# Ragged self-attention: a size class of 340 rows between 352 and 320

## The chip, the cores and the metric

The kernel runs on one core of a Trainium2 chip. The metric is the device time of one execution in microseconds (us); three runs of the kernel before took 351.78, 352.02 and 353.03 us, the median being 352.02 us. A separate execution was profiled; it took 353.66 us, of which 351.8 us lie between its first and its last instruction (the span).

The engines are called as in the profile: PE (TensorE, matmuls), DVE (VectorE), ACT (ScalarE), POOL (GpSimd), SP (SyncE, which here only starts transfers). PSUM is the memory that matmuls write to.

## The reference

A batch of 32 sequences, each of its own length between 64 and 511 rows, goes through one self-attention layer with 8 heads of 64. Rows beyond a sequence's length are zero in the output.

```python
for b in range(batch):                      # 32
    seq_len = lengths[b]
    x_b = x[b, :seq_len]                    # seq_len x 512
    q, k, v = np.split(np.matmul(x_b, w_qkv), 3, axis=-1)
    ...                                     # 8 heads of 64
    scores = 0.125 * np.matmul(q, k.transpose(0, 2, 1))
    attn = np.exp(scores - scores.max(-1, keepdims=True))
    attn = attn / (attn.sum(-1, keepdims=True) + 1e-08)
    output[b, :seq_len] = np.matmul(attn, v)...
```

The lengths are drawn with a fixed seed. Sorted, they are 502, 447, 446, 436, 363, 357, 351, 347, 343, 333, 323, 315, 310, 261, 260, 257, 246, 230, 223, 220, 216, 183, 164, 152, 143, 140, 134, 119, 101, 86, 79, 75.

## The kernel before, in words

**Sorting and classes.** At the start the kernel ranks the sequences by length, longest first, and takes them in pairs: ranks 0 and 1, 2 and 3, and so on, 16 pairs. A pair is worked with one code body, built for a class of N rows; the class is the smallest one that holds the longer sequence of the pair. The classes (`CLASSES`, L26) are the 15 multiples of 32 from 512 to 64. A table of the 16 pairs' classes is made on DVE (`class_table`, L881): it counts for each pair how many thresholds (all classes but the largest, written by POOL into `thr_f`, L1326) are not below its length. Each engine then reads its next class from that table (`next_class`, L923) and branches to the body.

With the lengths above the 16 pairs of the kernel before fall into the classes 512, 448, 384, 352, 352, 352, 320, 288, 256, 224, 224, 192, 160, 160, 128, 96. Pairs are numbered from 0 here, so pairs 3, 4 and 5 are the three of class 352; pair 5 holds the lengths 323 and 315, and pair 6, of class 320, the lengths 310 and 261.

**One half of a body.** A body has two halves, one for each sequence of the pair (`half`, L564). While PE does the attention of one sequence, it projects the next one between its steps, so each half holds the work of two sequences:

- Q0 to Q3 and K0 to K3 (small letters where ACT instead of DVE empties the bank): one of the four pairs of heads, 4 matmuls of N columns each (`qk`, L362);
- V: the value projection, here 4 matmuls of 512 columns for each of the T row tiles of 128 (`vtile`, L429);
- scores and their exponential, in one of two forms below;
- A0 to A3: attention times values, 18 matmuls of 65 columns for a pair of heads where T is 3 (`attnv`, L451), normalised by DVE into `onat`, which ACT and SP store.

What is projected in a half has W columns: N where the next sequence is of the same class, the next lower class where the kernel leaves the class (`leave`, L916).

**The two forms of scores where T is 3.** The ordinary form (`S` in the order string of L555, `scores`, L281) makes one key block of 128 keys at a time: two matmuls of N columns, one for each head of the pair, into one of two PSUM slots, then one exponential of 2N elements per partition on ACT. A half has 12 such steps. The dense form (`D` in L558, `scores_dense`, L325) lays all three key blocks of a head side by side in 1024 columns of PSUM, so 3N must not exceed 1024; both slots together hold a pair of heads. It makes 8 matmuls (each block that crosses the 512-column bank boundary is cut in two), then one exponential of 3N elements for each head. A half has 4 such steps. `is_dense` (L662) decides:

```python
def is_dense(N):
    return -(-N // P) == 3 and 3 * N <= 2 * MAXS      # P = 128, MAXS = 512
```

In the kernel before it holds for 320 and 288, not for 384 and 352. Each dense step first waits until ACT has emptied both slots; an ordinary step waits for its own slot alone.

**Code paths.** `graph` (L952) writes, for each class and engine, the blocks lead, first, again, last and tail. `first` holds the first half; a branch then goes to `again` (next pair of the same class, second half with W = N, back to `first`) or to `last` (second half with W of the next lower class, then `tail`, which branches to the lead of a lower class, or straight to `first` two classes down). On PE some of these blocks are put at chosen places within 256 instructions (`align`, L966), and branches get hints which way they will go. SP and POOL walk a plain chain of compares (`loops`, L941).

**Transfers.** SP starts, for each sequence, a load of its rows into `x_nat`; POOL casts to f16; SP starts one transposing DMA per row tile into `xT` (`to_xT`, L1160); PE waits on `s_xt` for them before it projects (`start_proj`, L570). Zeros for rows beyond the class's tiles are written from `zt`, also by SP.

Of the kernel before, what the change touches and what calls it, by code (L numbers as in the profile page):

```python
# [13 lines left out]
P = 128  # L14
# [5 lines left out]
STEP = 32  # L20
# [2 lines left out]
SECOND = {4: 20, 3: 60, 2: 0, 1: None}  # L23
AT_DENSE = 45
PIECE = 222
CLASSES = [STEP * k for k in range(16, 1, -1)]  # L26
FETCH = 256


# [109 lines left out]
def kernel(  # L139
# [9 lines left out]
    B, MAXS, D = x.shape  # L149
# [7 lines left out]
    def sb(name, shape, dt):  # L157
        return nc.alloc_sbuf_tensor(name, shape, dt).ap()
# [27 lines left out]
    rk_f = sb("rk_f", [B, NR], FP32)  # L186
    thr_f = sb("thr_f", [1, B // 2, len(CLASSES) - 1], FP32)
    ident_f = sb("ident_f", [P, P], FP32)
# [476 lines left out]
    def make_body(N, W, last=False):  # L665

        T = -(-N // P)
        pr = Prog(CANON, 0)
        st = {"slot": 0, "bank": 0}
        for h in range(2):  # L670
            st["x"] = False
            pr.add("dve", lambda e: set_now(e))
            half(pr, h, T, N, (N, W)[h], st, last and h == 1)
            pr.add("dve", lambda e: e.reg_add(rank_reg[0], rank_reg[0], 1))
            if h == 0:
                pr.second = {g: len(ops) for g, ops in pr.ops.items()}
        assert st == {"slot": 0, "bank": 0, "x": True}
        for b in banks:
            if not pr.busy[b]:
                pr.add("pe", lambda e, b=b: e.sem_inc(free[b], 1))  # L680
        assert not pr.signals
        return pr
# [3 lines left out]
    def set_now(e):  # L686
        rv = e.snap(rank_reg[0], min_val=0, max_val=B - 1)
        now[0] = masks[:, bass.ds(rv, 1), :, :].rearrange("p o a t -> p (o a) t")

    def make_bridge():  # L690
        pr = Prog(CANON, 0)
        acquire(pr, "a0")
        acquire(pr, "s1")
        pr.signals.append(s_xtf[0])
        scores(pr, 1, 0, 0, 0, 1, P)
        pr.add("pe", lambda e: e.sem_inc(free["a0"], 1))
        return pr

    def make_settled():

        pr = Prog(CANON)
        acquire(pr, "a1")
        pr.add("pe", lambda e: e.sem_inc(free["a1"], 1))
        return pr
# [176 lines left out]
    def class_table(e):  # L881
        q = Chain(e, s_self)
        q.tensor_tensor(
            out=thr_f,
            in0=n_s[0:1, 0:B:2].unsqueeze(2).broadcast_to([1, B // 2, len(CLASSES) - 1]),
            in1=thr_f, op=ALU.is_le,
        )
        q.reduce_sum(out=cls_f, in_=thr_f, axis=mybir.AxisListType.X)
        q.tensor_copy(out=cls[:, 0 : B // 2], in_=cls_f)
        q.memset(cls[:, B // 2 : B // 2 + 2], len(CLASSES))  # L890
        q.signal(s_cls)
# [21 lines left out]
        q.signal(s_tab)  # L913

    stay = {N: make_body(N, N) for N in CLASSES}
    leave = {N: make_body(N, max(N - STEP, CLASSES[-1])) for N in CLASSES}  # L916
    final = {N: make_body(N, max(N - STEP, CLASSES[-1]), True) for N in CLASSES if N <= P}
    bridge, settled = make_bridge(), make_settled()
    prologue = make_prologue()

# [2 lines left out]
    def next_class(e):  # L923
        r, k = regs[e.engine]
        e.reg_add(r, r, 1)
        if e.engine == nc.tensor.engine:
            k = regs["next"]
        e.reg_load(k, cls[0:1, bass.ds(e.snap(r, min_val=0, max_val=B // 2 + 1), 1)])

    def begin_loops(e):  # L930
        e.wait_ge(s_cls, 1)
        r, k = e.alloc_register("pair"), e.alloc_register("cls")
        e.reg_mov(r, 0)
        e.reg_load(k, cls[0:1, 0:1])
        regs[e.engine] = (r, k)
        if e.engine == nc.tensor.engine:
            regs["next"] = e.alloc_register("next")
            e.reg_add(r, r, 1)
            e.reg_load(regs["next"], cls[0:1, 1:2])

    def loops(e, name, body):  # L941
        r, cur = regs[e.engine]
        for k, N in enumerate(CLASSES):
            top = nc.cur_bb
            lab, out_ = f"{name}_b{k}", f"{name}_x{k}"
            e.br_cmp(cur, k, lab, out_, "IS_EQ")
            nc.switch_bb(lab, parent=top)
            body(e, N)
            e.br_cmp(cur, k, lab, out_, "IS_EQ")
            nc.switch_bb(out_, parent=top)  # L950
# [136 lines left out]
    def wait_dec(e, s, n=1):  # L1087
        e.wait_ge(s, n)
        e.nop().then_inc(s, -n)  # L1089
# [39 lines left out]
    with nc.Block() as block:  # L1129

        @block.sync
        def _(e):
# [27 lines left out]
            def to_xT(h, N):  # L1160
                T = -(-N // P)
                for t in range(T):
                    tile_to_xT(h, t, min(P, N - t * P))
                if T < NT:
                    e.nop().then_inc(s_xt[h], 16 * (NT - T))

            def tile_to_xT(h, t, n):
                e.dma_start_transpose(
                    out=xT[h][:, :, t * P : t * P + n], in_=x16[h][0:n, t, :]
                ).then_inc(s_xt[h], 16)  # L1170
# [141 lines left out]
        @block.gpsimd  # L1312
        def _(e):
            def iota(o, pattern, base, mult, last=False):
                ins = e.iota(o, pattern=pattern, base=base, channel_multiplier=mult,
                             allow_small_or_imprecise_dtypes=True)
                if last:
                    ins.then_inc(s_iota, 1)

            iota(pos_f, [[-1, B]], B - 1, 0)  # L1320
            iota(pos_c, [[0, 1]], B - 1, -1)
            iota(rk_f[:, 0:B], [[1, B]], 0, 0)
            iota(rk_f[:, B:NR], [[0, NR - B]], B - 1, 0)
            iota(sel[:, 1, :], [[0, P]], 0, 1)
            iota(row_f, [[P, NT]], 0, 1)
            iota(thr_f, [[0, B // 2], [-32, len(CLASSES) - 1]], CLASSES[0] - 32, 0, True)  # L1326
            q = Chain(e, s_pself)
            q.memset(ident_f, 0.0)
            q.affine_select(
                out=ident_f, in_=ident_f, compare_op=ALU.not_equal, fill=1.0,  # L1330
                base=0, pattern=[[-1, P]], channel_multiplier=1,
            )
            q.join()
            e.tensor_copy(out=ident, in_=ident_f).then_inc(s_id, 1)
            rank = e.alloc_register("rank")
            e.reg_mov(rank, 0)

            def cast(h, T):
                wait_dec(e, s_xl[h], 16)
                e.tensor_copy(out=x16[h][:, 0:T, :], in_=x_nat[h][:, 0:T, :]).then_inc(  # L1340
                    s_xc[h], 1
                )

            def ones(h, T, src):
                e.tensor_copy(  # L1345
                    out=v_aug[h][:, 0:T, :, HD],
                    in_=src[:, 0, 0:T].unsqueeze(2).broadcast_to([P, T, NH]),
                ).then_inc(s_on[h], 1)

            def fill(i, a):  # L1350
                e.memset(ep32[:, i, a], 0.01).then_inc(s_ini, 1)  # L1351


            e.wait_ge(s_c0[NT - 1], 1)
            fills = [(i, a) for i in range(1, NPAIR) for a in range(2)]
            for i, a in fills:
                fill(i, a)
            for t in range(2):
                e.wait_ge(s_x1[t], 16)
                e.tensor_copy(out=x16[1][:, t, :], in_=x_nat[1][:, t, :]).then_inc(s_xc[1], 1)  # L1360
            e.wait_ge(s_tab, 1)
            ones(0, NT, masks[:, B, :, :])
            e.wait_ge(s_c1[NT - 1], 1)
            e.memset(qkT[1].bitcast(FP32)[:, 1 : 2 * NPAIR : 2, :], 0.0).then_inc(s_ini, 1)
            e.wait_ge(s_tab, 2)
            wait_dec(e, s_x16f[0])
            cast(0, NT)
            begin_loops(e)

            def body(e, N):  # L1370
                T = -(-N // P)
                for h in range(2):
                    wait_dec(e, s_vf[1 - h])
                    rv = e.snap(rank, min_val=0, max_val=B - 1)
                    ones(1 - h, T, masks[:, bass.ds(rv, 1), :, :].rearrange(
                        "p o a t -> p (o a) t"))
                    wait_dec(e, s_x16f[1 - h])
                    cast(1 - h, T)
                    if h == 0:
                        next_class(e)  # L1380
                    e.reg_add(rank, rank, 1)

            loops(e, "pool", body)
# [89 lines left out]
```

## Time and profile before

| what | value |
|---|---|
| runs, us | 351.78, 352.02, 353.03 (median 352.02) |
| profiled execution, us | 353.66 |
| its span, us | 351.8 |
| PE busy | 332.7 us, 95% of the span |
| ACT busy | 246.4 us, 70% |
| DVE busy | 198.7 us, 56% |
| POOL busy | 60.4 us, 17% |
| mean granted TensorE clock | 0.990 |

"Busy" is the time in which an engine has an instruction under way. A row of the costliest groups gives line, engine, operation, output and input tiles, shape and count, then busy time and the mean of one instruction, then the idle time of the engine just ahead of them and what ended it. A table of stretches gives the busy time of each engine between two moments of the span. A row of the timeline gives the start, the time taken, the instructions merged into it and, in brackets, the idle time before it.

### The profile page before, as it was taken

The numbers are of one execution on the slowest core, as the hardware profiler recorded it, in microseconds if no ns is written. First come the engines' busy times: TensorE is split into PE (matmuls) and PEld (weight loads), VectorE is DVE, ScalarE is ACT, GpSimd is POOL, SyncE is SP. The second block draws the span as 40 slices with busy tenths as digits, with TensorE's granted clock in tenths as the row PEclk, the third lists the DMA queues.
The fourth block names the chain that finished last, engine by engine and source line by source line (L and its number), as shares of the span: only waits on it lengthen the run. The fifth ranks groups of instructions, "written<-read, shape, count | busy, mean of one in ns | idle before, by whom it ended". The sixth has DMA issues, their size and how long they took to land. (4 is left out here: it accounts for less than half of the span.)

```text
span 351.8 us, 11327 instructions
## 1 busy us (share of the span) xinstructions
PE 332.7 (95%) x3982; PEld 203.5 (58%) x3983; DVE 198.7 (56%) x442; ACT 246.4 (70%) x355; POOL 60.4 (17%) x90
## 2 busy tenths in 40 slices
PE   7799999999999999999999999999999999996972
PEld 2565445555545565555555566667677777664751
DVE  3576566666645445354354555655756667664652
ACT  4468778777768888988888877788675766553431
POOL 2534020202010111011011022201121122120120
PEclk9999999999999999999999999999999999999898
DMA  6957989866677496897678679899799687765632
GB/s 206 346 138 265 276 273 253 244 212 167 204 174 259 110 314 229 160 308 263 175 251 303 168 211 311 248 254 170 200 196 197 178 177 196 175 199 167 130 107 68
DMA packets 83462, 74.57 MB, mean 212 GB/s; under 512 B 40640, under 2 KB 63168, under 8 KB 83392
## 3 DMA queue, kind: packets, MB, share of 16 engines
q1 hardware_dynamic: 71536, 62.15, 65.6%
q10 hardware_dynamic: 11856, 11.54, 9.6%
q8 instruction: 37, 0.61, 0.8%
q14 instruction: 33, 0.27, 0.2%
HBM read 27.80 MB, written 36.70 MB: 183 GB/s over the span
## 5 line engine op out<-in xcount | busy, mean ns | idle before, releaser
L321 ACT ACTIVATE ep<-psc 128x704 f16<-128x704 f32 (+7 forms) x217 | 172.4, 845 | 61.9 <-PE psc L279 46.2
L279 PE MATMUL pa<-xT,w_r 128*128 128x352 f16 (+14 forms) x1056 | 155.3, 281 | 7.7 <-PEq L55 6.1
L279 PEld LDWEIGHTS pa<-xT,w_r 128*128 128x128 f16 x1056 | 83.7, 99 | 54.2 <-issue 22.5
L388 DVE CAST qkT<-pa 128x512 f16<-128x512 f32 (+8 forms) x96 | 54.2, 566 | 70.9 <-PE pa L279 70.4
L279 PE MATMUL pa<-w_r,xT 128*128 128x512 f16 (+2 forms) x384 | 83.2, 349 | 0.3 <-DVE v_aug L443 0.3
L279 PE MATMUL pav<-v_aug,ep 128*128 128x65 f16 x1792 | 77.4, 194 | 0.0
L279 PEld LDWEIGHTS pav<-v_aug,ep 128*128 128x128 f16 x1792 | 70.0, 98 | 11.9 <-issue 1.7
L279 PE MATMUL psc<-qkT 64*128 64x352 f16 (+14 forms) x686 | 65.8, 291 | 1.1 <-ACT ep L321 0.5
L443 DVE TENSOR_TENSOR v_aug<-pa,masks 128x512 f16<-128x512 f32 (+1 forms) x76 | 51.4, 677 | 22.2 <-PE pa L279 19.8
L386 ACT CAST qkT<-pa 128x352 f16<-128x352 f32 (+6 forms) x92 | 41.8, 454 | 21.4 <-ACTq L55 14.4
L524 DVE SCALAR_TENSOR_TENSOR onat<-pav,masks,rcp 128x256 f32<-128x256 f32 (+2 forms) x128 | 52.0, 444 | 5.4 <-DVE rcp L500 1.6
L1345 POOL CAST v_aug<-masks 128x24 f16 (+4 forms) x33 | 9.1, 276 | 255.7 <-POOLq L1089 255.7
L279 PEld LDWEIGHTS pa<-w_r,xT 128*128 128x128 f16 x384 | 31.4, 98 | 32.1 <-issue 6.6
L1340 POOL CAST x<-x_nat 128x1536 f16<-128x1536 f32 (+3 forms) x33 | 42.1, 1275 | 14.3 <-POOLq L1089 14.1
L279 PEld LDWEIGHTS psc<-qkT 64*128 64x128 f16 x686 | 23.1, 94 | 34.5 <-issue 29.1
L500 DVE RECIPROCAL rcp<-pav 128x8 f32<-128x8 f32 (+1 forms) x68 | 14.6, 214 | 37.0 <-PE pav L279 21.3
L353 ACT ACTIVATE ep<-psc 128x864 f16<-128x864 f32 (+2 forms) x32 | 27.7, 918 | 7.6 <-PE psc L279 6.5
L522 DVE TENSOR_TENSOR onat<-pav,rcp 128x512 f32<-128x512 f32 (+2 forms) x32 | 17.8, 558 | 1.1
L708 PE MATMUL psc<-zt 128*128 128x512 f16 x22 | 7.5, 499 | 1.7 <-DVE zt L1405 1.7
L778 ACT CAST w_r<-w_f 128x512 f16<-128x512 f32 (+1 forms) x6 | 4.4, 758 | 4.2 <-DMA w_f<-in_w_qkv_dram 4.2
L1351 POOL MEMSET ep<- 128x1024 f32 x6 | 5.4, 955 | 9.1 <-DVE x L769 9.1
L708 PEld LDWEIGHTS psc<-zt 128*128 128x128 f16 x22 | 2.4, 119 | 4.7 <-issue 2.4
(59 smaller groups left out, 35.4 us busy)
## 6 DMA issues: line engine op xcount, KB each, us to landing
out_dram<-zt SPq DMA_DIRECT2D x16, 768.0 KB, 6.1
x_nat<-in_x_dram SPq DMA_DIRECT2D x12, 768.0 KB, 5.0
x_nat<-in_x_dram SPq DMA_DIRECT2D x7, 1024.0 KB, 5.8
x_nat<-in_x_dram SPq DMA_DIRECT2D x11, 512.0 KB, 4.3
out_dram<-onat ACTq DMA_DIRECT2D x12, 384.0 KB, 5.4
out_dram<-onat SPq DMA_DIRECT2D x12, 384.0 KB, 3.9
out_dram<-onat ACTq DMA_DIRECT2D x16, 256.0 KB, 4.2
out_dram<-zt SPq DMA_DIRECT2D x12, 256.0 KB, 4.4
```

The lines of the kernel that those rows point to most:

```text
L279: return lambda e: e.matmul(o, lhsT, rhs, start=start, stop=stop)
L321: lambda e: e.activation(out=dst, in_=src, func=AF.Exp, scale=scale),
L353: lambda e, par=par, b=b: e.activation(out=ep[:, i, par, 0:3, 0:N], in_=psc_f[:, par, 0 : 3 * N].rearrange("p (t n) -> p t n", n=N), func= ...
L386: group(pr, b, eng, mms, lambda e: e.copy(out=dst, in_=src))
L388: group(pr, b, eng, mms, lambda e: e.tensor_copy(out=dst, in_=src))
L443: lambda e: e.tensor_tensor(out=v_aug[h][:, t, lo // HD : lo // HD + n, 0:HD], in0=pa[:, bank, 0:w].rearrange("p (a d) -> p a d", d=HD), i ...
L500: pr.add("dve", lambda e: e.reciprocal(out=rv, in_=den).then_inc(s_r, 1))
L522: ins = e.tensor_tensor(op=ALU.mult, **ops)
L524: ins = e.scalar_tensor_tensor(scalar=now[0][:, 1, t : t + 1], op0=ALU.mult, op1=ALU.mult, **ops)
L708: e.matmul(psc[:, 1, 0, :], zt16[:, 0:P], zt16[:, 0:MAXS], start=True, stop=True)
L1340: e.tensor_copy(out=x16[h][:, 0:T, :], in_=x_nat[h][:, 0:T, :]).then_inc(s_xc[h], 1)
L1345: e.tensor_copy(out=v_aug[h][:, 0:T, :, HD], in_=src[:, 0, 0:T].unsqueeze(2).broadcast_to([P, T, NH]),).then_inc(s_on[h], 1)
```

## The change

A sixteenth class of 340 rows is put between 352 and 320. 340 is the largest N for which 3N (1020) fits 1024 columns, so `is_dense` holds for it. With it:

- pair 5 (lengths 323 and 315) goes to class 340 instead of 352. No other pair changes its class: the next lower pair, with 310, stays in 320;
- the second half of pair 4, which stayed in class 352 and projected 352 columns, now leaves the class and projects 340; the two halves of pair 5 take the dense form, the first projecting 340 columns and the second 320;
- the next lower class of each class is looked up in a table (`lower`) instead of N - 32;
- transposes still move a multiple of 32 rows (96 in the last tile of 340, as for 352), so their number and sizes stay;
- the thresholds are written by three iota instructions on POOL instead of one, since their spacing is no longer even; the table has 16 x 15 entries instead of 16 x 14;
- every engine gets the code of one more class.

```diff
-CLASSES = [STEP * k for k in range(16, 1, -1)]
+DENSE_ROWS = 340
+CLASSES = sorted([STEP * k for k in range(2, 17)] + [DENSE_ROWS], reverse=True)
...
     stay = {N: make_body(N, N) for N in CLASSES}
-    leave = {N: make_body(N, max(N - STEP, CLASSES[-1])) for N in CLASSES}
-    final = {N: make_body(N, max(N - STEP, CLASSES[-1]), True) for N in CLASSES if N <= P}
+    lower = dict(zip(CLASSES, CLASSES[1:] + CLASSES[-1:]))
+    leave = {N: make_body(N, lower[N]) for N in CLASSES}
+    final = {N: make_body(N, lower[N], True) for N in CLASSES if N <= P}
...
             def to_xT(h, N):
                 T = -(-N // P)
                 for t in range(T):
-                    tile_to_xT(h, t, min(P, N - t * P))
+                    tile_to_xT(h, t, min(P, -(-N // STEP) * STEP - t * P))
...
-            iota(thr_f, [[0, B // 2], [-32, len(CLASSES) - 1]], CLASSES[0] - 32, 0, True)
+            at = CLASSES.index(DENSE_ROWS)
+            for a, b in ((1, at), (at, at + 1), (at + 1, len(CLASSES))):
+                iota(thr_f[:, :, a - 1 : b - 1], [[0, B // 2], [-STEP, b - a]], CLASSES[a], 0,
+                     b == len(CLASSES))
```

## The prediction, made before the changed kernel was run

> **What bounds the kernel now.** I read the page's busy shares first, then a table of stretches over the six halves around the change, then PE's own waits, then the timeline of one dense half.
>
> ```profile
> PE 332.7 (95%) x3982; PEld 203.5 (58%) x3983; DVE 198.7 (56%) x442; ACT 246.4 (70%) x355; POOL 60.4 (17%) x90
> ```
>
> PE is busy 95% of the span. Busy alone doesn't prove that PE is the limit, so the stretches come next. I cut them where a half begins on PE: in class 352 at its V1 (found as the middle of the eight 512-column matmuls that hold V0 and V1), in the dense classes at the first dense step.
>
> ```profile
> core 0: us, PE busy (x) PEld busy (x) DVE busy (x) ACT busy (x) POOL busy (x), PEclk, DMA share, GB/s
> 164.28:176.91 12.63, 12.63 (x142) 6.99 (x141) 5.72 (x13) 10.22 (x19) 1.70 (x2) 1.00 0.75 243
> 176.91:189.54 12.63, 12.63 (x142) 7.00 (x141) 6.08 (x13) 10.93 (x20) 1.70 (x2) 1.00 0.72 238
> 189.54:202.33 12.79, 12.32 (x141) 6.80 (x140) 6.18 (x15) 10.61 (x19) 1.70 (x2) 1.00 0.78 231
> 202.33:213.99 11.66, 11.66 (x149) 7.54 (x150) 6.40 (x13) 8.96 (x12) 1.76 (x2) 1.00 0.68 202
> 213.99:225.28 11.29, 11.23 (x150) 7.54 (x150) 6.34 (x14) 8.66 (x12) 1.76 (x2) 1.00 0.92 270
> 225.28:236.32 11.04, 11.04 (x150) 7.48 (x150) 6.86 (x15) 8.38 (x13) 1.76 (x2) 1.00 1.02 291
> ```
>
> The rows are: second half of pair 4 (N 352, W 352); pair 5 (352/352, then 352/320); pair 6 of class 320 (W 320, then 288); first half of pair 7 of class 288. In every row PE's busy time equals the stretch but for 0.47 and 0.06 us, at the full clock of 1.00; ACT has 1.7 to 2.7 us to spare. So here the length of a half is the length of PE's matmul stream, and PE's waits say where that stops being true:
>
> ```profile
> PE pa L279 <- PEq L55: 6.1, 4, 3.5
> PE psc L279 <- ACT ep L321: 0.5, 1, 0.5
> ```
>
> The second row is the 0.47: the first dense step after an ordinary half, which needs both slots. The 6.1 us lie at the end, in the classes of 160 rows and less. Since PE hardly stops between 27 us and 308 us, what is saved on PE in the middle should arrive at the end.
>
> **The change part by part.** All is summed against the profiled execution (353.66 us, span 351.8); its own time is 1.64 us over the median of the runs, and I carry the difference over to the median, 352.02.
>
> *Pair 5's first half, ordinary to dense.* Before: 12.63. After: N and W are 340. Row 320/320 has 11.66 and row 288/288 has 11.04, so 32 rows of a dense half cost 0.62 and 20 rows 0.39: 12.05. It is not the 32 matmuls' columns that make most of the gain; a half of 352 against one of 320 differs by 0.97, against 0.62 for the same 32 rows within the dense form, so the form itself is worth 0.35.
>
> *Pair 5's second half.* Before 12.79 with the wait of 0.47. After: N 340, W 320. From 320/288 (11.29) the 32 more projected columns add 0.37 (11.66 less 11.29), and the 20 more rows of dense scores add 20/32 of (0.62 - 0.37), 0.16: 11.82.
>
> *Pair 4's second half now leaves the class.* Before 12.63. The nearest row is the leaving half 352/320 with its wait, 12.79; 20 more projected columns add 20/32 of 0.37, 0.23. The wait moves here from pair 5. It is paced by ACT, whose last two ordinary exponentials of the half grow from 640 to 680 elements:
>
> ```profile
> L321 ACT ACTIVATE ep<-psc 128x704 f16<-128x704 f32 x72 | 50.8, 756 | 8.6 <-PE psc L279 8.2 <-ACTq L55 0.4
> L321 ACT ACTIVATE ep<-psc 128x640 f16<-128x640 f32 x19 | 12.5, 701 | 9.3 <-PE psc L279 6.5 <-ACTq L55 2.8
> L353 ACT ACTIVATE ep<-psc 128x864 f16<-128x864 f32 x16 | 13.4, 888 | 3.4 <-PE psc L279 3.0 <-ACTq L55 0.2
> L353 ACT ACTIVATE ep<-psc 128x960 f16<-128x960 f32 x14 | 12.8, 968 | 3.8 <-PE psc L279 3.5
> ```
>
> 64 elements are 55 ns there, so 40 are 34 ns, two 0.07: 13.09. Queued behind that wait is all of PE's work; nothing else waits for it before PE does.
>
> Sum of the three halves: before 12.63 + 12.63 + 12.79 = 38.05, after 13.09 + 12.05 + 11.82 = 36.96: 1.09 less.
>
> *ACT inside the dense half.* A dense step's two exponentials of 1020 elements: 96 elements cost 80 ns (968 less 888), so one is 1.02 us and the pair 0.10 longer than at 320. It is hidden under PE except where the steps lie closest, third to fourth:
>
> ```profile
> 208.59 0.58 PE L279 MATMUL psc<-qkT 64*128 64x320 f16 x8
> 209.20 0.97 ACT L353 ACTIVATE ep<-psc 128x960 f16<-128x960 f32 x1
> 210.07 0.96 ACT L353 ACTIVATE ep<-psc 128x960 f16<-128x960 f32 x1
> 211.18 0.59 PE L279 MATMUL psc<-qkT 64*128 64x320 f16 x8
> ```
>
> From one start to the next are 2.59 us; ACT ends at 211.03, so its cover is 0.15, about what a signal takes here (in the next half the fourth step comes 0.15 after ACT's end, with 0.06 idle on PE). At 340 PE's own work between the two grows by about 0.10 in the first half and 0.03 in the second, ACT's chain by 0.12: at most 0.1 more per half. Bounds 0 and 0.2 for both; I take 0.05, nearer the idle of 0.06 that the trace has in that place.
>
> *Prologue.* The one iota over 224 entries takes 0.68 us and ends at 2.47; the others take 0.12 to 0.25. Two more cost at most 0.5, nearer 0.2. DVE's first sort step, which waits for it, starts at 3.05 on the landing of the lengths: hidden, cover 0.58. POOL's later identity ends at 3.61 and PE uses it at 8.6. The two DVE steps over the threshold table (0.37 each for 224) grow by 16/224, 0.05 together, and this does lie on the path: PE's first 512-column projection at 16.78 waits 1.04 for the DVE copies behind them. Cost 0.05.
>
> *Code.* One more body is entered and left on each engine. PE's code comes in blocks over a queue of its own; from 200 to 216 us, the entry, branch and rest of class 320:
>
> ```profile
> q8 instruction: 2, 0.03, 0.9%
> ```
>
> Two blocks, and PE's only idle there is the 0.47 counted above. I cost the new body at 0, because class 320 is the same shape of visit (lead, first, last), hidden by instructions already queued at PE; uncovered, 0.9% of 16 us on 16 engines is 1.15 us per block. On SP, loads, transposes, stores and zero fills keep their number and size; on POOL the casts too. SP starts the three transposes at 204.35 in class 320 and they land by about 211 (the last start, 208.7 less 1.3, plus the median landing of 3.3), while PE first needs them at 214.5: a cover over 3 us.
>
> Total: 1.09 - 0.05 - 0.05 = 0.99. 352.02 - 0.99 gives **351.0** us (0.28% less; the profiled execution's own would be 352.7). A difference under about 0.5%, 1.76 us, is what a measurement of this kernel can hardly tell from none.
>
> **The rivals.**
>
> *End stalls move.* The largest of PE's late waits is before a projection at 128 columns:
>
> ```profile
> 324.41 1.86 PE L279 MATMUL pa<-xT,w_r 128*128 128x128 f16 x16 [3.50 <-PEq L55]
> xT<-x SPq DMA_TRANSPOSE x1, 4.9
> ```
>
> The second row, from the stretch 320.46 to 324.41, is the transpose that it waits for: 4.9 us to landing against a median of 3.3, minimum 2.3 and maximum 5.9. [...] The whole tail comes 1 us earlier and its transfers may interleave otherwise. At the minimum, 2.6 come off: 348.4; at the maximum, 1.0 is added: 352.0. For it: the three runs spread over 1.25 us. Against it: everything in the tail is paced by PE and moves together.
>
> *The gain is eaten in the dense steps.* If each of the new halves' eight steps showed ACT's added 0.10 on PE, 0.8 is lost less the 0.05 counted: 351.8. Against it: between the other steps ACT has 0.23 us and more.
>
> *Code blocks are exposed: slower.* If PE stood for the new body's two blocks at its branch and its entry, 2.3 us at 1.15 each, the time is 353.3; with the longest block of the whole trace, 2.26 us at 282.8, 4.5 us, 355.5. Above 0.99 us exposed the change loses; above 2.75 it is slower by over 0.5%. For it: the extra branches are certain. [...]
>
> *No pair is in the new class.* Then 352.0. Against it: lengths 323 and 315 are in the draw, and the 72 exponentials of 704 elements are what three pairs of class 352 make (6 halves of 9, 3 from the half before, 5 times 3 from the next sequence).
>
> **How the numbers follow.** Forecast 0.60, with 350.3 to 351.7 as its own range (gain 0.3 to 1.7: the uncertainty of the extrapolated halves, 0.2, and the spread of the runs). End stalls: 0.14 downwards, 0.05 upwards. Eaten: 0.10. Code: 0.10, half of it beyond 353.8. No pair: 0.01. Faster by over 0.5% (below 350.26): the downward stalls and the forecast's lower edge, 0.20. Slower by over 0.5% (above 353.78): the code case's upper half and some of the upward stalls together with the runs' spread, 0.09. Within: 0.71. The range reaches down into the first rival to 349.6 and up to 352.8, where about 0.1 is left out on either side.
>
> **What would show it.** In the profile after: 14 dense exponentials of 1020 elements, 16 of 960 and 3 ordinary ones of 680; 48 of 704 instead of 72; three stretches near 13.1, 12.05 and 11.8; the idle of about 0.5 before the first dense step at 340, none before the first at 320. Idle at PE ahead of the branch or the lead of class 340 would be the code case; idle before the fourth dense step over 0.1 the eaten case. Wrong altogether would be a tail (from class 160 on) whose length changes by more than the middle's 1 us.

## The result, and the profile after

The changed kernel takes 349.84 us (median of 22 runs, 347.86 to 354.64) against 352.55 us (22 runs, 351.04 to 356.44) for the kernel before: ratio 0.992, 95% interval 0.990 to 0.994. It is 2.7 us faster. A few executions of each kernel come out 1.5% or more above its fastest; ratios and intervals leave them out, medians and ranges hold them. The forecast was 351.0 with 1.0 us of gain. The measured time lies below the forecast's own range (350.3 to 351.7) and inside the whole one (349.6 to 352.8), which reaches that far down only for the rival of the end stalls; 1.7 us of the gain are not in the sum.

First the table of stretches of the changed kernel, over the same three halves as before (second half of pair 4, then pair 5):

```profile
core 0: us, PE busy (x) PEld busy (x) DVE busy (x) ACT busy (x) POOL busy (x), PEclk, DMA share, GB/s
163.29:176.38 13.09, 12.56 (x142) 6.84 (x141) 6.31 (x15) 10.84 (x19) 1.70 (x2) 1.00 0.82 238
176.38:188.44 12.06, 12.06 (x149) 7.51 (x150) 6.45 (x13) 9.39 (x12) 1.76 (x2) 1.00 0.71 211
188.44:200.27 11.83, 11.78 (x149) 7.51 (x150) 6.50 (x15) 9.18 (x12) 1.76 (x2) 1.00 0.83 253
```

They were forecast at 13.09, 12.05 and 11.82. Together they are 36.98 instead of 38.05 us: 1.07 less. The timeline of the changed kernel has the wait where it was expected, ahead of the first dense step at 340, and its groups of exponentials by shape have the expected counts:

```profile
176.38 0.61 PE L280 MATMUL psc<-qkT 64*128 64x340 f16 x8 [0.53 <-ACT ep L322]
```

```profile
L322 ACT ACTIVATE ep<-psc 128x704 f16<-128x704 f32 x48 | 33.9, 756 | 6.3 <-PE psc L280 5.6 <-ACTq L56 0.4 <-issue 0.2
L354 ACT ACTIVATE ep<-psc 128x960 f16<-128x960 f32 x16 | 14.7, 968 | 3.8 <-PE psc L280 3.3 <-ACTq L56 0.2
L354 ACT ACTIVATE ep<-psc 128x1020 f16<-128x1020 f32 x14 | 13.5, 1018 | 3.8 <-PE psc L280 3.4
L322 ACT ACTIVATE ep<-psc 128x680 f16<-128x680 f32 x3 | 2.1, 733 | 0.4 <-ACTq L56 0.4
```

The rest of the gain is at the end. From the first dense step of class 288 on, the two kernels do the same work. I cut both there, at PE's long wait in the leaving half of class 160 (it projects 128 columns for the first sequence of class 128), and at the end of the span. Before:

```profile
225.28:320.91 95.63, 94.25 (x1271) 68.67 (x1270) 62.33 (x142) 62.26 (x92) 17.79 (x26) 1.00 0.85 200
320.91:324.41 3.50, 0.00 (x1) 0.03 (x2) 0.45 (x1) 1.20 (x2) 0.26 (x1) 1.00 0.52 158
324.41:351.83 27.42, 18.39 (x296) 14.03 (x296) 12.48 (x26) 8.12 (x13) 4.37 (x9) 0.87 0.41 105
```

After:

```profile
223.22:318.94 95.72, 94.33 (x1271) 68.61 (x1270) 62.36 (x142) 62.23 (x92) 17.81 (x26) 1.00 0.88 197
318.94:321.19 2.25, 0.00 (x1) 0.04 (x2) 0.44 (x1) 1.19 (x2) 0.26 (x1) 1.00 0.66 226
321.19:346.88 25.69, 16.77 (x296) 12.54 (x296) 12.40 (x26) 8.12 (x13) 4.37 (x9) 0.94 0.41 113
```

The first rows agree to 0.09 us. The wait is 1.25 us shorter, and what follows it is 1.73 us shorter with the same 296 matmuls (PE busy 18.39 and 16.77). The column after the engines, PEclk, tells why: 0.87 against 0.94. In the 3.41 us right behind the wait it was 0.50 before (324.41 to 327.82) and 1.00 after (321.19 to 324.60). In the timeline of before the matmuls there are slow, in that of after they are not:

```profile
324.41 1.86 PE L279 MATMUL pa<-xT,w_r 128*128 128x128 f16 x16 [3.50 <-PEq L55]
326.06 1.09 PE L279 MATMUL pav<-v_aug,ep 128*128 128x65 f16 x16
326.96 1.03 PE L279 MATMUL pa<-xT,w_r 128*128 128x128 f16 x8
327.93 0.42 PE L279 MATMUL psc<-qkT 64*128 64x160 f16 x8
```

```profile
321.19 1.05 PE L280 MATMUL pa<-xT,w_r 128*128 128x128 f16 x16 [2.25 <-PEq L56]
322.08 0.65 PE L280 MATMUL pav<-v_aug,ep 128*128 128x65 f16 x16
322.56 0.61 PE L280 MATMUL pa<-xT,w_r 128*128 128x128 f16 x8
323.11 0.42 PE L280 MATMUL psc<-qkT 64*128 64x160 f16 x8
```

From the first to the fourth start are 3.52 us before and 1.92 after: 1.60 lost at the lower clock. So of the profiled executions' difference (353.66 less 348.69, 4.97) 1.07 lie in the middle and 2.89 behind it. Nearly all of the rest, 0.95, is in the prologue: PE's fourth group of 512-column scores starts at 28.30 before and at 27.35 after. I take that for chance, since five later kernels with before's prologue have 27.1 to 27.5 there. The runs' medians, 2.71 apart, leave about 1.6 for the tail.

What PE waits for there is `xT`, the transposes that SP starts. The timelines of SP, just ahead of the long wait, before and after (start, time taken):

```profile
316.21 0.41 SPq L1174 DMA_DIRECT2D x_nat<-in_x_dram  x1
318.11 2.52 SPq L1168 DMA_TRANSPOSE xT<-x  x2
321.76 0.41 SPq L1097 DMA_DIRECT2D out_dram<-onat  x1
323.23 0.40 SPq L1174 DMA_DIRECT2D x_nat<-in_x_dram  x1
```

```profile
314.02 0.40 SPq L1176 DMA_DIRECT2D x_nat<-in_x_dram  x1
315.47 2.51 SPq L1170 DMA_TRANSPOSE xT<-x  x2
319.03 0.40 SPq L1099 DMA_DIRECT2D out_dram<-onat  x1
320.50 0.40 SPq L1176 DMA_DIRECT2D x_nat<-in_x_dram  x1
```

From load to load SP needs 7.02 us before and 6.48 after, for the same transfers; PE's three halves ahead of this (301.52 to 320.46 before) take 6.3 each. So SP is the slower of the two at the end, and its lead over PE runs out at class 160. In the kernel before the two transposes start 1.49 us after the load has been issued, in the changed one 1.05. In this gap SP of the kernel before stands twice with nothing to wait for that the trace shows, 0.37 and 0.24 us (at 317.0 and 317.9). Such a pause also comes at 254.3 and 294.0 (0.36, 0.39); the changed kernel has two of 0.39 up to this point, at 263.4 and 300.5.

### The profile page after: what moved, and what is told of

It reads as the page before. It is cut to its first block, busy times and chain, and to the rows that moved or that the text cites. A ratio compares the mean times of both kernels' runs of the same rounds, so it can differ in the third digit from the quotient of the medians.

```text
span 346.9 us, 11368 instructions
## 1 busy us (share of the span) xinstructions
PE 329.4 (95%) x3998; PEld 202.9 (58%) x3999; DVE 200.5 (58%) x446; ACT 244.1 (70%) x343; POOL 60.8 (18%) x92
## 5 line engine op out<-in xcount | busy, mean ns | idle before, releaser
L322 ACT ACTIVATE ep<-psc 128x704 f16<-128x704 f32 (+7 forms) x193 | 155.6, 857 | 58.0 <-PE psc L280 43.3
L280 PE MATMUL pa<-xT,w_r 128*128 128x224 f16 (+15 forms) x1056 | 153.2, 279 | 6.5 <-PEq L56 5.0
L389 DVE CAST qkT<-pa 128x512 f16<-128x512 f32 (+9 forms) x100 | 56.2, 563 | 64.9 <-PE pa L280 63.9
L280 PEld LDWEIGHTS pav<-v_aug,ep 128*128 128x128 f16 x1792 | 69.2, 98 | 12.1 <-issue 1.9
L280 PE MATMUL psc<-qkT 64*128 64x352 f16 (+17 forms) x702 | 64.9, 287 | 1.2 <-ACT ep L322 0.5
L387 ACT CAST qkT<-pa 128x352 f16<-128x352 f32 (+7 forms) x88 | 39.9, 453 | 19.2 <-ACTq L56 11.4
L354 ACT ACTIVATE ep<-psc 128x960 f16<-128x960 f32 (+3 forms) x48 | 43.1, 949 | 11.3 <-PE psc L280 9.7
L280 PEld LDWEIGHTS psc<-qkT 64*128 64x128 f16 x702 | 24.0, 94 | 33.4 <-issue 27.8
```

Source lines behind the costliest of these rows:

```text
L280: return lambda e: e.matmul(o, lhsT, rhs, start=start, stop=stop)
L322: lambda e: e.activation(out=dst, in_=src, func=AF.Exp, scale=scale),
L354: lambda e, par=par, b=b: e.activation(out=ep[:, i, par, 0:3, 0:N], in_=psc_f[:, par, 0 : 3 * N].rearrange("p (t n) -> p t n", n=N), func= ...
L387: group(pr, b, eng, mms, lambda e: e.copy(out=dst, in_=src))
L389: group(pr, b, eng, mms, lambda e: e.tensor_copy(out=dst, in_=src))
```

## The experiments

Three theories stand in the first four expectations: L, that the new code as such (its place on the engines) brings the rest; S, that the tail gains because it is reached 1 us earlier; N, that the runs merely spread.

**The class is there but never visited.** Changed kernel with:

```diff
+    lower[352] = 320
...
-                iota(thr_f[...], [[0, B // 2], [-STEP, b - a]], CLASSES[a], 0,
+                iota(thr_f[...], [[0, B // 2], [-STEP, b - a]], CLASSES[a] if a != at else 320, 0,
```

> The changed kernel with two edits: the threshold of the class of 340 is written as 320, so that no pair reaches it, and the half that leaves class 352 projects 320 columns again. The matmuls, exponentials and transfers that are executed are those of the kernel before; only the code of a sixteenth class (unused), the three iotas and the longer threshold table are there. Measured so far: the change gains 2.7 us (0.8%), of which PE's three changed halves explain 1.07. Theory L (the rest of the gain comes from the new code itself, by where it puts the other engines' instructions or by a later start of some transfers): 1.6 us faster than before, ratio 0.995. Theory S (the rest comes from the tail and the transfers being reached 1 us earlier): no change, ratio 1.000. Theory N (the rest is the spread of runs): no change, ratio 1.000.

Measured: 352.52 against 353.1, ratio 0.9986 (0.9947 to 1.0024). Its twelve runs lie in two groups, four from 349.5 to 350.1 and eight from 352.0 to 354.5. I first read this as the end of L. That was too quick, as the next set shows.

**The class is visited, in the ordinary form.** Changed kernel with `is_dense` false for 340:

```diff
-        return -(-N // P) == 3 and 3 * N <= 2 * MAXS
+        return -(-N // P) == 3 and 3 * N <= 2 * MAXS and N != DENSE_ROWS
```

> The changed kernel with the class of 340 rows worked in the ordinary form of scores: rows alone, without the dense form. By the prediction's rows the two halves of the pair cost about 12.4 (12.63 less 20/32 of 0.37) and 12.2 instead of 12.05 and 11.82, the wait of 0.5 before the first dense step goes back to the entry of class 320, and pair 4's second half is 12.4: the three halves make about 37.5 with that wait, 0.5 less than before (38.05). Theory L: 2.1 us faster than before (0.5 and the 1.6 of the code), ratio 0.994. Theories S and N: 0.5 us faster and no more than that by much, ratio 0.998 to 0.999.

Measured: ratio 0.992 (0.9887 to 0.9953), though its middle is only 0.45 shorter than before's (60.63 against 61.08; the middle runs from the fifth of the eight value matmuls in pair 4's second half, at 164.20 before, to the first dense step of 288). The dense form isn't what brings the rest.

**Before, shortened in class 320.** Five of the value projection's twelve matmuls are left out where `short` holds, in the first half of class 320, so the output is not the reference's:

```diff
+        if short:
+            mms = mms[:1] + mms[2 if i == 1 else 3 :]
```

> The kernel before, with 5 of the 12 value-projection matmuls of 512 columns left out in the first half of class 320 (so the values of that one sequence are incomplete): PE is 5 times 0.215 us = 1.08 us shorter in the middle, as with the change, but no class is added and the code of no other engine moves. Theory S: the whole gain of the change comes out, 2.7 us, ratio 0.992. Theories L and N: 1.1 us, ratio 0.997.

Measured: ratio 1.0002 (0.997 to 1.0034), but its middle was 61.46, not shorter: PE gained a wait of 0.47 behind ACT's exponentials in this half, and one of 0.43 in the next whose end the profile lays to nothing. The tail was not reached earlier, so this says nothing on S.

**After, lengthened by as much as it gains.** K0 and Q0 are done twice where `twice` holds, in the first half of 340:

```diff
+        if twice:
+            mms = mms + mms
```

> The changed kernel, with the four matmuls of 340 columns of K0 and of Q0 each done twice in the first half of class 340 (the second time over the first, so nothing is changed but time): 8 times 0.145 us = 1.16 us are added on PE, a little more than the 1.07 that the changed halves gained. Theory L: still 1.5 us faster than before, ratio 0.996. Theories S and N: back to the time before, ratio 1.000.

Measured: 350.64, ratio 0.994 (0.9911 to 0.9968), with a middle of 61.16, 0.08 longer than before's. The middle takes as long as before and the kernel is still 2 us faster: from the first dense step of 288 to the end its profile has 123.7 us, like the changed kernel's (123.7) and unlike before's (126.6). S falls, and with this and the earlier kernel N does too.

**Only SP gets more code.** The kernel before, with one more body of three tiles on SP, never entered, at the place where class 340 would stand (its transposes' sizes rounded up as in the changed kernel, which alters no class that is visited):

```diff
-        for k, N in enumerate(CLASSES):
+        todo = list(enumerate(CLASSES))
+        if name == "sp":
+            todo.insert(CLASSES.index(320), (len(CLASSES) + 3, 340))
+        for k, N in todo:
```

> The kernel before, with the code of one more body (that of class 340) put on SP between classes 352 and 320, behind a compare that never holds. So SP's code for the classes from 320 down stands where the changed kernel has it; everything else is as before. Two theories of the 1.7 us that the change brings beyond the 1.07 of the middle. C: SP's code has moved, and with it the places where SP stands for its next code (0.36 to 0.41 us each; in the kernel before three of them lie at 254.3, 294.0 and 317.0 us, in the changed kernel two, at 263.4 and 300.5), in a stretch from about 248 to 325 us where SP starts transfers with no pause and PE at last waits for its transposes. By C this kernel takes about 1.7 us less than the kernel before: 351.2, ratio 0.995, and in its trace SP's pauses lie as in the changed kernel. V: it takes a visit to the new class, by something that is not SP's code. By V the ratio is 1.000. The kernel that has the new class but never visits it came out at 0.9986 (0.9947 to 1.0024), so C is doubtful and something between the two, 0.998, would not surprise.

Measured: 350.69 (six runs, 349.13 to 350.92), ratio 0.9925 (0.9901 to 0.995). Code that never runs makes the kernel before about as fast as the changed one, with a middle of 61.09. Its pauses on SP lie as in the changed kernel (0.41, 0.40, none close ahead of class 160's leaving half), and its timeline of SP shows 6.51 us from load to load:

```profile
315.36 0.40 SPq L1177 DMA_DIRECT2D x_nat<-in_x_dram  x1
316.81 2.50 SPq L1171 DMA_TRANSPOSE xT<-x  x2
320.37 0.40 SPq L1100 DMA_DIRECT2D out_dram<-onat  x1
321.87 0.40 SPq L1177 DMA_DIRECT2D x_nat<-in_x_dram  x1
```

**The reverse: the changed kernel without a new body on SP.** SP works class 340 with the body of 352, which starts the same transfers:

```diff
+            if name == "sp" and N == DENSE_ROWS:
+                continue
...
+                if name == "sp" and k + 1 == CLASSES.index(DENSE_ROWS):
+                    e.br_lt(cur, k + 2, lab, out_)
```

> The changed kernel, but SP works class 340 with its body of class 352 (the two start the same transfers, three tiles each), so SP has as much code as before, in the same places; PE, ACT, DVE and POOL are as in the changed kernel and visit class 340. By C the extra 1.7 us are lost again: 351.5, ratio to the kernel before 0.997, and SP's pauses are three as before. By V it is as fast as the changed kernel: 349.8, ratio 0.992.

Measured: 352.95 against 353.02, ratio of the compared runs 0.9962 (0.9919 to 1.0006): the middle's gain (60.02 instead of 61.08, 1.06 less) and little else. The interval overlaps the changed kernel's own, so this alone would not decide; the timeline points the same way. The pause is back ahead of the critical transposes, as before, and SP needs 7.24 us from load to load. (This profile also has a wait of PE of 1.51 us at 46.5 us, ahead of all places where SP's code differs; five of the 14 profiles have one of 1.3 to 1.9 there, the fastest kernel's among them, so a single profile's total says little.)

```profile
315.43 0.41 SPq L1185 DMA_DIRECT2D x_nat<-in_x_dram  x1
317.32 2.52 SPq L1179 DMA_TRANSPOSE xT<-x  x2
321.19 0.41 SPq L1108 DMA_DIRECT2D out_dram<-onat  x1
322.67 0.40 SPq L1185 DMA_DIRECT2D x_nat<-in_x_dram  x1
```

**The code of the other engines, without SP's.** The unvisited class of the first run, with the edit on SP of the last one:

> The changed kernel with class 340 never visited (its threshold written as 320, and 320 as the class below 352), as in the first of the runs, and with no body for it on SP: so SP's code is as long as before and stands where it stood before, while PE, ACT, DVE and POOL carry the code of a class that no pair uses. It is the complement of the kernel before with one more body on SP alone, which came out at 0.9925. The kernel with the unused class on every engine came out at 0.9986. If the places of the code add up engine by engine (SP's gives 0.75%, the others' cost 0.6%, by which of PE's code loads fall on SP's transposes), this one is slower than the kernel before: 1.004 to 1.008, 354.3 to 355.7 us. If the 0.9986 was low by chance, or the other engines' code costs nothing: 1.000, with 0.997 to 1.002 as bounds.

Measured: ratio 0.9981 (0.9945 to 1.0016). The new code on PE, ACT, DVE and POOL neither costs nor brings anything that can be told.

**Filling the wait with matmuls.** Is the lowered clock part of the price? Eight matmuls on constants (`WARM` is 8) were first put ahead of class 128's first projection, in both kernels:

```diff
         if T == 1:
+            if N == P and h == 0:
+                acquire(pr, f"a{st['bank']}")
+                pr.add("pe", lambda e, k=st["bank"]: [
+                    e.matmul(pa[:, k, :], w_r[:, 0, 0:P], w_r[:, 0, 0:MAXS], start=True, stop=True)
+                    for _ in range(WARM)
+                ])
             start_proj()
```

> The kernel before, with eight matmuls of 512 columns on constant data (about 1.75 us) ahead of the first projection of class 128, into a bank that this projection overwrites. In the profile before, PE stood there 3.50 us for a transpose, and its clock was then 0.72 on average over the next 6 us; these matmuls fill half of the wait and shorten nothing else. Theory D: the stall of over 3 us costs a lowered clock (about 1.6 us), and the gain beyond 1.07 is that the changed kernel stalls 2.25 and keeps its clock. By D this kernel is faster by up to 1.6 us: 351.3 to 351.9, ratio 0.9955 to 0.9975, and its records show a clock of 1.00 behind that wait. If the lowered clock is not the price, or comes from elsewhere: ratio 1.000.

> The changed kernel with the same eight matmuls. By D little is left to gain, since its stall there is 2.25 us and the clock holds: 349.6 to 349.9, ratio to the kernel before 0.991 to 0.992, so that it is now only 1.1 to 2.0 us faster than the kernel before with the same matmuls, instead of 2.7. If the clock is not the price: 349.8 as well, but 2.7 to 3 us faster than the kernel before with these matmuls.

Measured: 0.9996 (0.9968 to 1.0024) and 0.9942 (0.9919 to 0.9965). The place was wrong: the long wait is one half earlier, and in the first of them it stood untouched at 2.58 us, with the added matmuls at 327.59 behind it. They tell one thing: about 1.75 us of extra PE work at that place costs the kernel before nothing that can be told, so PE isn't the bound there; for the changed one 0.9942 stands against 0.992, and the intervals overlap. The same matmuls were then put where the wait is, in the kernel before (the lines left out are those of the eight matmuls):

```diff
             else:
+                if T == 2 and W <= P and not st["x"]:
...
                 start_proj()
```

> The kernel before with the eight matmuls of 512 columns on constant data (1.75 us) put where the long wait is: in the leaving half of class 160, ahead of its first projection (the earlier pair of runs had them one half later, behind the wait). PE's wait of 3.50 us becomes work of 1.75 and a wait of 1.75; nothing else is shortened. Theory D (the lowered clock behind a wait of over 3 us is part of the price): 351.3 to 352.0, ratio 0.9955 to 0.998, and a clock of 1.00 behind the wait. Without D: 1.000, or more where the wait of a run is below 1.75.

Measured: 351.49 against 352.61, ratio 0.9968 (0.9939 to 0.9996). Work without a result made the kernel 1.1 us faster, by an interval that ends just below 1. Its timeline shows the matmuls behind the shortened wait at their full speed (compare 1.86 and 1.09 before):

```profile
321.46 1.90 PE L626 MATMUL pa<-w_r 128*128 128x512 f16 x8
324.69 1.05 PE L280 MATMUL pa<-xT,w_r 128*128 128x128 f16 x16 [1.33 <-PEq L56]
325.58 0.65 PE L280 MATMUL pav<-v_aug,ep 128*128 128x65 f16 x16
```

**SP's chain shortened.** One of two compares per half is asked only if the other one holds, in both kernels:

```diff
-                    nc.switch_bb(out_, parent=top)
-                    lab, out_ = f"more_b{N}_{h}", f"more_x{N}_{h}"
+                    lab = f"more_b{N}_{h}"
                     e.br_lt(rank, B // 2 - EARLY, lab, out_)
```

> The kernel before with one branch less per half on SP: the second question on zero fills (is the rank below 14) is asked only where the first (is it below 16) was answered yes, instead of always, so the same transfers start in the same order. In the trace such a compare with its jump takes 0.16 to 0.17 us on SP. Theory P: from 248 to 325 us SP starts transfers back to back and is what PE waits for, and what shortens SP's chain there shortens the time. 13 halves lie on it: 2.1 us less for SP, of which the time takes what PE waited: 350.7, ratio 0.994, or 349.3 (0.990) if a lowered clock behind the long wait goes as well. If SP's chain isn't what sets the time, and only the places of its code or the collisions with other loads matter: between 0.998 and 1.002. The code of SP becomes shorter by two instructions per body, so its pauses move too; the trace will tell how many lie in the stretch.

> The changed kernel with the same edit on SP. By P the 2.1 us are worth what is left of PE's waits in classes 160 and below (2.25, 0.41, 0.89 and 0.74 in its profile): 347.5 to 348.5, ratio to the kernel before 0.985 to 0.988, and the distance to the kernel before with this edit shrinks from 2.7 towards the 1.07 of the middle (1.0 to 1.6), since neither waits long any more. If SP's chain isn't what sets the time: 349.8, ratio 0.992, and the distance stays 2.7.

Measured: 1.0009 (0.9977 to 1.004) and 0.9904 (0.9874 to 0.9933, median 348.89). For the kernel before that is a miss. SP's compares and short gaps did fall by 2.05 us between the last transpose of the three-tile classes (241.16 before) and the last of the two-tile ones (326.16), but this chain stayed 85.2 us long (85.0 before). First, up to about 281 us SP now comes too early and waits; the waits of SP from 262 to 300 us, first before, then with the edit:

```profile
SPq L1089 <- SPq L1089: 0.4, 2, 0.2
```

```profile
SPq L1089 <- SPq L1089: 1.5, 3, 0.8
```

Second, one pair of transposes shortly ahead of the critical half took 1.0 us longer than usual:

```profile
309.24 3.51 SPq L1168 DMA_TRANSPOSE xT<-x  x2
```

Third, the late pause (0.37 and 0.24, at 316.4 and 317.2) stayed. The last of the critical transposes now started 2.35 us ahead of PE's need instead of 1.51, but a store of ACT's started 1.30 us behind it, it landed after 4.8 us (the last section has the count), and PE still waited 2.58. So what counts on SP is the stretch from its last wait, at about 281 us, to the critical transposes; lead gained before that is given back. With the same edit the changed kernel came out at 348.89, the lowest median of all, but its interval overlaps the changed kernel's 0.990 to 0.994, so it can't be called faster than that.

## Why the prediction was right, and where not

*The three halves* were right to 0.02 us each: scaling from 320 and 288 rows carried to 340. (The 0.05 for the prologue can't be told from its chance spread.) *ACT inside the dense step* was right: the two dense halves stand at 12.06 and 11.83, and the second shows 0.05 of idle (0.05 was taken). *The code on PE* costs nothing, as forecast: no idle at the branch or the lead of 340, and the unvisited code on the engines other than SP measured 0.9981. The rivals of an eaten gain and of no pair in the class fall with the rows above.

*The step that failed* is the last of the part on code: SP's new body was costed at nothing, because its transfers keep their number and size and PE needs them over 3 us later. That cover was read at 214.5 us, in class 320, and it holds there. It is gone at 320 us, where PE already waited 3.50 for these transfers. The forecast had quoted this wait, and had set against the rival of the end stalls that "everything in the tail is paced by PE and moves together". From load to load SP's 6.48 to 7.02 us against PE's 6.3 say that it isn't. That rival had 0.14 downwards, with 348.4 as its time, so direction and size were near the mark; its mechanism was right by half. It said that the tail gains by coming 1 us earlier and meeting other transfers. The lengthened kernel after excludes the first. The second is there: the transpose that PE waits for landed after 4.87 us before, after 4.30 in the changed kernel and after 2.33, the rival's minimum, in the kernel before with one body more on SP. That the measured time still fell into the whole range is owed to this rival's share of it and partly to luck, since its reason was another. What the runs showed in the failed step's place is the place of SP's code, which shifts its pauses: with SP's new places but no class the kernel gains 2.6 us, and with the class but SP's old places it gains 1.3.

The prediction named one finding that would make it "wrong altogether": a tail that changes by more than 1 us. It changed by 2.9 in the profiled executions, and about 1.6 in the medians. By its own measure the forecast had the middle right and the tail wrong.

Set side by side, each kernel's gain in us ((1 - ratio) times 352.6), less what its middle gained; then from its one profile the tail (from the first dense step of 288 to the end; before has 126.6) and how much of it PE ran at half clock ahead of the last halves (before: 3.4):

| SP's code | kernel | gain | of it middle | beyond | tail | low clock |
|---|---|---|---|---|---|---|
| new places | changed | 2.8 | 1.1 | 1.7 | 123.7 | 0 |
| | ordinary form at 340 | 2.8 | 0.5 | 2.4 | 123.3 | 0 |
| | lengthened | 2.1 | -0.1 | 2.2 | 123.7 | 0 |
| | before, one body more on SP | 2.6 | 0.0 | 2.6 | 124.9 | 0 |
| | changed, one compare less | 3.4 | 1.1 | 2.3 | 123.3 | 0 |
| | class never visited | 0.5 | 0.0 | 0.5 | 126.3 | 3.4 |
| old places | changed, SP shares a body | 1.3 | 1.1 | 0.3 | 125.2 | 0 |
| | class never visited, none on SP | 0.7 | 0.0 | 0.7 | 128.3 | 6.8 |
| | before, one compare less | -0.3 | 0.0 | -0.3 | 126.5 | 3.4 |
| | before, shortened | -0.1 | -0.4 | 0.3 | 127.7 | 6.8 |

The three kernels with added matmuls are left out; in the two with one compare less SP's code is also shorter by two instructions a body, so their places are new or old only nearly. Each gain is uncertain by 0.7 to 1.6 us (the ratios' intervals). The kernel whose class is never visited stands out: its SP code lies in the new places, and only four of its twelve runs show the gain. In its trace from 260 us on four SP transposes take 1.85 to 2.17 us instead of 1.24, and PE's clock was lowered behind a wait of 2.0. That is the edge of what went with a lowered clock in the 14 traces (1.99 us and more in a window, last section), so its runs may fall on either side; why this kernel comes to that edge and the others with the new places don't is open.

The chain from the pauses to the time has two links. The first is the wait at class 160, where PE needs the second of two transposes. That one starts 1.51 us ahead of PE's need before (319.40) and 2.19 ahead after (316.75), and lands 4.87 and 4.30 us after its start: of the 1.25 us of difference 0.68 are SP's lead and 0.57 a quicker landing. The second is PE's clock behind a long wait, 1.6 us lost before and 0 after. The matmuls in the wait bear it out (0.9968): the granted clock of that kernel's compared executions is 0.993 to 0.998, that of the kernel before timed beside it 0.987 to 0.995, so the clock isn't lowered in every run before, which fits a gain of 1.1 and not 1.6.

The second link can be there without the first. The tails of the kernel before and of the kernel before with one body more on SP, as wholes:

```profile
225.28:351.83 126.55, 112.64 (x1567) 82.74 (x1566) 75.26 (x168) 71.58 (x106) 22.41 (x36) 0.97 0.75 178
```

```profile
224.19:349.04 124.85, 110.87 (x1567) 81.16 (x1566) 75.19 (x168) 71.56 (x106) 22.36 (x36) 0.98 0.71 180
```

PE is not busy for 13.91 us in the one and for 13.98 in the other. In place of waits of 0.32, 0.40, 3.50 and 1.86 stand five of 0.41 to 1.89; the 1.70 gained are the 1.77 of busy time for the same matmuls, that is the clock. In the changed kernel 1.36 less of idle time comes on top. That SP's pauses are waits for its next code is only argued: they move with its code and back.

## What to carry to other kernels

Code that was never run moved the time here by as much as the change did (one more body on SP alone 2.6 us, the changed kernel 2.8 by its ratio), with an engine that issues transfers and had no lead left: before a small gain is credited to a change, give the kernel before the same amount of code and time that. Read the cover of a transfer in every stage, above all in the last, where the lead of the issuing engine had run down here (over 3 us in class 320, a wait of 3.50 at class 160); the wait that the profile shows there is where these small shifts arrived. The wait of 3.50 us on PE cost 1.6 us more than itself, while as much idle time in the tail (13.98 us against 13.91) with no wait over 1.89 did not, and eight matmuls put into the long wait brought 1.1 us (0.9968, by an interval that ends just below 1).

## What the runs showed of the hardware

**How long PE had stood idle where its clock was lowered.** In the traces' record of the granted clock the low spells last 3.41 us or twice that, at 0.5 (but for the last one, which runs into the end). In the kernel before the clock is 1.00 from 7.00 to 324.44, 0.50 to 327.85, 1.00 to 348.33 and 0.50 to the end; in the changed kernel it is 1.00 from 5.80 to 343.72 and 0.50 to the end. The four spells that end inside the span are 93, 1, 6 and 99 times 3.413 us long, so I count in windows of that length, back from a spell's start. In the 14 traces, every window from 250 us on in which PE stood idle for 1.99 us or more was followed by a low spell (in the tail ahead of the last halves: 2.00, 2.05, 2.09, 2.15 and 3.38), and no window at full clock with 1.89 or less was. By this count it matters how a wait lies on these windows: one of 3.18 us, cut into 1.73 and 1.45, left the clock at 1.00, and one of 2.58 us, with 2.09 in one window, did not. The stretches of 3.41 us behind these two waits, the first in the changed kernel whose SP shares a body, the second in the kernel before with one compare less:

```profile
323.45:326.86 3.41, 2.99 (x54) 2.51 (x55) 2.08 (x6) 1.41 (x3) 1.04 (x1) 1.00 0.69 193
```

```profile
323.59:327.00 3.41, 3.41 (x51) 2.89 (x52) 1.84 (x5) 0.80 (x2) 1.04 (x1) 0.69 0.71 201
```

**The critical transpose landed late where a store started close behind it.** These are the landings of the critical transpose in the changed kernel and in the kernel before with one body more on SP (before: the 4.9 us in the prediction), and ACT's store next to it before and in these two:

```profile
xT<-x SPq DMA_TRANSPOSE x1, 4.3
```

```profile
xT<-x SPq DMA_TRANSPOSE x1, 2.3
```

```profile
319.88 0.44 ACTq L1097 DMA_DIRECT2D out_dram<-onat  x1
```

```profile
317.93 0.38 ACTq L1099 DMA_DIRECT2D out_dram<-onat  x1
```

```profile
319.95 0.38 ACTq L1100 DMA_DIRECT2D out_dram<-onat  x1
```

The store starts 0.47, 1.18 and 1.87 us behind the transpose's start. In the 14 traces the transpose landed after 2.32 or 2.33 us in the four where the store started 1.35 or more behind it, and after 3.75 to 4.87 in the ten where it started 1.30 or less behind it. The same holds where PE first projects for a lower class, at 44 to 47 us: 2.5 us in the nine traces where ACT's store started 2.0 or more behind the last transpose, 4.1 to 4.4 in the five with 1.2 to 1.5, and only these five have the wait of 1.3 to 1.9 there. So at these two places a few tenths of SP's lead may decide about 2 us. This is counted; no kernel here moved ACT's store alone. It does not hold at every place: in the kernel before, the second transposes of the two halves just ahead, at 305.83 and 312.46, landed after 2.47 and 2.33 us with ACT's store 1.32 and 1.21 behind them.

**Slow transposes on SP and PE's code loads.** Queue q8, of kind "instruction", carries 37 loads of 16 KB in the kernel before, about one for every 225 instructions of PE, and none from 154.1 to 193.8 us, where the body of class 352 is repeated; I read it as PE's code. Issuing a transpose took SP 1.25 us there (median of 80), but in the 14 traces, from 60 us on, 150 of the 236 that overlapped a load on q8 of over 0.7 us took more than 1.35 us (mean 1.66, up to 2.74); of the 744 that overlapped none on that queue 18 did (mean 1.26). In the kernel before alone these are 8 of 14 and 3 of 56, in the changed one 10 of 21 and 0 of 49. The longest pair of the kernel before, in SP's timeline, with the queues in the same stretch:

```profile
282.75 4.04 SPq L1168 DMA_TRANSPOSE xT<-x  x2
```

```profile
q8 instruction: 1, 0.02, 5.0%
```

This is a coincidence counted, not a cause tried: no kernel here moved PE's code loads alone onto the transposes or off them.
